# The state update of a head as one product over 128 rows: u and V share a tile, odd pairs put their outputs on the straight column half, and no state burst is cut in two

## The chip, the cores and the metric

The kernel runs on one core of a Trainium2 chip. The metric is the device time of one execution in microseconds. A core has a matrix engine (TensorE, "PE" in the profile, with its weight loads as "PEld"), a vector engine (VectorE, "DVE"), a scalar engine (ScalarE, "ACT"), a general one (GpSimd, "POOL"), and a sync engine (SyncE, "SP"), whose queue issues nearly all transfers of this kernel, in order. SBUF is the on-chip memory and PSUM the one that TensorE writes its sums to; both have 128 partitions.

## What is computed

One layer of a hybrid trunk for 512 tokens and 16 learned meta tokens ahead of them, width 2048. A normalised input goes through one projection whose columns feed two groups; group A has 16 heads of 64 with a recurrence over time, group B a gated convolution of width 3. Both are gated, go through one output projection, and the residual and a last norm follow. Cut to what matters here:

```python
Pr, Pc = (rmsnorm(h_res) @ w_in)[..., :RW_COLS], ...    # w_in: 2048 x 8320
# group A, for each head (N = 64), state S is N x N:
def step(S, inp):
    r_t, w_t, k_t, v_t, kk_t, b_t = inp
    sa = einsum('bhvk,bhk->bhv', S, kk_t)
    S = S * w_t[:, :, None, :] - sa[..., None] * b_t[:, :, None, :] + v_t[..., None] * k_t[:, :, None, :]
    y_t = einsum('bhvk,bhk->bhv', S, r_t)
    return S, y_t
y_a = (groupnorm(y) * lnx_g + lnx_b + bonus) * silu(g_r)
# group B
y_b = Bg * causal_conv_w3(Cg * hc) * silu(g_c)
out = rmsnorm(h_res + concat(y_a, y_b) @ w_out)
```

## The kernel before

**Tiles and stages.** The sequence is cut into 9 chunks of 64 (`NCH`): chunk 0 holds the meta tokens, 1 to 8 the real ones. The 16 heads are 8 pairs (`NPAIR`); a pair fills 128 partitions, head `h` the half `hs`, with `ho` for the other half. A pair i has the place `(i % 2) * 4 + i // 2`, so places 0 to 3 are the even pairs (e = 0) and 4 to 7 the odd ones (e = 1).

Instead of stepping through time, the kernel prepares each chunk of each head in closed form. `prepare` builds the operands of a pair, `invert` the inverse X of a triangular 64 x 64 matrix per chunk, and both write them to a tensor in device memory, `opd`, of one row per partition: 576 columns (`OPW`) hold AR, KK, BR, X, V and B' (offsets `O_AR` to `O_B`). V and B' come from transposes on VectorE (L922 and L824) whose 32 x 32 blocks are put in place by the transfers that `stash_later` issues (L902 to L908, L917 to L922, issued at L678). B' of a head has 128 rows, 64 that meet u and 64 that meet V, in two column pieces of 32 steps each, interleaved (`bb` in `recur`).

`recur` then runs the recurrence, chunk after chunk, all 16 heads at once. `load_chunk` (L1040) brings the operands of a chunk and a pair into the tile `ct`, 288 KB. For each chunk c:

- the products A·S and K·V into the PSUM tiles `z` (named rz; L1063), for even pairs in `z[0]` straight (rows and columns on the same half) and for odd pairs in `z[1]` crossed;
- ScalarE negates them into `pn` (L1071); filler for 2900 ns; the product with X (L1080) gives u in the other half of `z`; ScalarE and VectorE copy it to `u`, one each (L1083, L1084); filler for 2900 ns;
- the state burst. Its two lists are `here` and `there`. `here`: the state update into the PSUM tile `zs`, per head two products over 64 rows, B'·u and B'·V, straight (L1118); then, for the last odd pair, its three output products, into `z[0]`. `there`: the outputs `zy` of the other seven pairs, three products each (with the state, V and u), crossed (L1122). One step issues one entry of each list for both heads, so four products, one on each quadrant (a half of the rows with a half of the columns). In chunk 7 (`NCH - 2`) filler of 1000 ns is put in the middle of the burst. Chunk 0 has no outputs, chunk 8 no state update;
- the loads of chunk c+2 for the first four pairs (those of chunk c+1 for the other four stand behind `pn`); VectorE forms the new state (L1130, L1131); `norm` does the group norm of the outputs, seven heads of a column half from `zy` and one from `z[0]`, and writes them to `yd`; filler for 4200 + 1000 ns (4200 in chunk 7).

**What sets the order.** TensorE's order is the order of the code. `fill(ns)` takes as many matmuls of the input projection from the generator `mains` (tiles `ps_*`, L350 and L365) as last that many nanoseconds, and `until` takes them up to a certain result. So the projection's matmuls stand between all bursts of `prepare`, `invert` and `recur`. On the other engines a scheduler sorts by priority; `ahead()` lifts an instruction's priority. Weights of the projection come in halves of 512 KB into three buffers (`wr`, L157, on SP's queue); ScalarE casts each to a rounded high part (L149), VectorE subtracts to get the low part (L150), into six buffers (`w`), and TensorE takes them in turn. `later(ns, fn)` puts a transfer into the code once that much filler has been issued.

After the recurrence, `split_mix` reads `yd` back (the odd offset for the last place, L1207, is due to its straight outputs), and the output projection follows.

Of the kernel before, what the change touches and what calls it, by code (L numbers as in the profile page):

```python
# [89 lines left out]
def hymba_kernel(ctx: ExitStack, tc: tile.TileContext, xt, xtok, front, w_in, w_out, pv, lup, cst, msk, gf, out):  # L90
# [13 lines left out]
    opd = [dp.tile([NCH * P * OPW], F32, tag=f"opd{j}", name=f"opd{j}", bufs=1) for j in range(NPAIR)]  # L104
    rbd = [dp.tile([P, SEQ], F32, tag=f"rbd{j}", name=f"rbd{j}", bufs=1) for j in range(NPAIR)]
    gated = [dp.tile([P, SEQ], F32, tag=f"gated{j}", name=f"gated{j}", bufs=1) for j in range(NPAIR)]
    yd = dp.tile([2 * NPAIR * CH, SEQ], F32, tag="yd", name="yd", bufs=1)
    mixd = {j: dp.tile([P, SEQ], F32, tag=f"mixd{j}", name=f"mixd{j}", bufs=1) for j in range(NPAIR, KT)}

# [483 lines left out]
    def later(ns, fn):  # L593
        pending.append((clock[0] + ns, fn))
        pending.sort(key=lambda e: e[0])
# [89 lines left out]
    def stash_later(ns, *a):  # L685
        later(ns, lambda: stash(*a))
# [4 lines left out]
    def prepare(i):  # L691
# [209 lines left out]

        for h, hs, ho in heads:  # L902
            for b in range(2):
                for t in range(2):
                    stash_later(
                        9000 + 900 * (4 * h + 2 * b + t), i, bt[64 * h + 32 * b : 64 * h + 32 * b + 32, :, t].rearrange("p c s a -> p c (s a)"),
                        O_B + 64 * b, 64, 64 * h + 32 * t, 32, 0, NCH - 1,
                    )  # L908
# [7 lines left out]
        nc.vector.transpose(vs.rearrange("p c s -> p (c s)"), v)  # L916
        for b in range(4):  # L917
            for t in range(2):
                stash_later(
                    14000 + 1000 * (2 * b + t), i, vs[32 * b : 32 * b + 32, :, 32 * t : 32 * t + 32], O_V + 32 * (b % 2), 32,  # L920
                    64 * (1 - b // 2) + 32 * t, 32,
                )  # L922
        fill(FW["vt"])
        return dict(gt=gt, xT=xT, xo=xo, i=i)

# [112 lines left out]
            fill(FW["lev"] if level is level_a else FW["begin"])  # L1038

    def load_chunk(ch, c, pairs, ops):  # L1040
        n = OPW if c < NCH - 1 else O_B
        for i in pairs:
            t = ch.tile([P, OPW], F32, tag=f"ct{i}", name=f"ct{i}_{c}", bufs=2)
            nc.sync.dma_start(t[:, 0:n], spot(i, 0, P, c, 1, 1, 0, n))
            ops[c, i] = t

    def recur(ch):
        ops = {}  # L1050
        load_chunk(ch, 0, range(NPAIR), ops)
        load_chunk(ch, 1, range(NPAIR), ops)
        st = None
        for c in range(NCH):
            last = c == NCH - 1
            z = [pz.tile([P, 2, 4, CH], F32, tag="tz", name=f"rz{c}_{e}") for e in range(2)]
            for k in range(4):
                for part in range(0 if c else 1, 2):
                    for e in range(2):
                        t = ops[c, 2 * k + e]  # L1060
                        o = O_KK if part else O_AR
                        for h, hs, ho in heads:
                            nc.tensor.matmul(  # L1063
                                z[e][ho if e else hs, 0, k], t[hs, o : o + CH],
                                t[hs, O_V : O_V + CH] if part else st[hs, 4 * e + k],
                                start=(part == 0 or c == 0), stop=(part == 1),
                            )
            pn = ch.tile([P, 2, 4, CH], F32, tag="pn", name=f"pn{c}", bufs=2)
            with ahead():
                for e in range(2):  # L1070
                    nc.scalar.activation(pn[:, e], z[e][:, 0], AF.Copy, scale=-1.0)  # L1071
            if c and not last:
                load_chunk(ch, c + 1, range(4, NPAIR), ops)
            fill(FW["p"])
            for k in range(4):
                for e in range(2):
                    t = ops[c, 2 * k + e]
                    for h, hs, ho in heads:
                        m = ho if e else hs
                        nc.tensor.matmul(z[e][hs, 1, k], t[m, O_X : O_X + CH], pn[m, e, k], start=True, stop=True)  # L1080
            u = ch.tile([P, 2, 4, CH], F32, tag="u", name=f"u{c}", bufs=2)
            with ahead():
                nc.scalar.copy(u[:, 0], z[0][:, 1])  # L1083
                nc.vector.tensor_copy(u[:, 1], z[1][:, 1])  # L1084
# [6 lines left out]
            for k in range(4):  # L1091
                for e in range(2):
                    t, j = ops[c, 2 * k + e], 4 * e + k
                    if not last:
                        bb = t[:, O_B : O_B + 2 * CH].rearrange("p (s a) -> p a s", a=2)
                        here += [(zs, j, bb[:, 0], 0, u[:, e, k], 0, 2), (zs, j, bb[:, 1], 0, t[:, O_V : O_V + CH], 1, 2)]
                    if c and j < NPAIR - 1:
                        there += [
                            (zy, j, st[:, j], O_AR + CH, t, 0, 3),
                            (zy, j, t[:, O_V : O_V + CH], O_KK + CH, t, 1, 3),  # L1100
                            (zy, j, u[:, e, k], O_BR, t, 2, 3),
                        ]
                    elif c:

                        here += [
                            (z[0][:, 0], 0, t, O_AR + CH, st[:, j], 0, 3),
                            (z[0][:, 0], 0, t, O_KK + CH, t[:, O_V : O_V + CH], 1, 3),
                            (z[0][:, 0], 0, t, O_BR, u[:, e, k], 2, 3),
                        ]
            steps_ = max(len(here), len(there))  # L1110
            for n in range(steps_):
                if c == NCH - 2 and n == steps_ // 2:
                    fill(FW["mid"])
                if n < len(here):
                    d, j, t, o, x, a, b = here[n]
                    for h, hs, ho in heads:
                        w = t[hs, o : o + CH] if o else t[hs]
                        nc.tensor.matmul(d[hs, j], w, x[hs], start=(a == 0), stop=(a == b - 1))  # L1118
                if n < len(there):
                    d, j, x, o, t, a, b = there[n]  # L1120
                    for h, hs, ho in heads:
                        nc.tensor.matmul(d[ho, j], t[hs, o : o + CH], x[hs], start=(a == 0), stop=(a == b - 1))  # L1122
            if c + 2 < NCH:
                load_chunk(ch, c + 2, range(0, 4), ops)
            if not last:
                new = ch.tile([P, NPAIR, CH], F32, tag="st", name=f"st{c}", bufs=2)
                scale = dd[:, c].unsqueeze(2).to_broadcast([P, NPAIR, CH])
                with ahead():
                    if c:
                        nc.vector.tensor_tensor(out=new, in0=zs, in1=st, op=ALU.add)  # L1130
                    nc.vector.tensor_tensor(out=new, in0=new if c else zs, in1=scale, op=ALU.mult)  # L1131
                st = new
            if c:
                norm(ch, (zy, z[0][:, 0, 0:1]), c)
            fill(FW["s"] if c == NCH - 2 else FW["s"] + FW["mid"])


    def norm(ch, zs, c):
# [4 lines left out]
        def spread(j):  # L1143
            return nv[:, j].unsqueeze(2).to_broadcast([P, NPAIR, CH])

        for z, j in zip(zs, (slice(0, NPAIR - 1), slice(NPAIR - 1, NPAIR))):
# [49 lines left out]
    def split_mix(j):  # L1196
# [4 lines left out]
        if j < NPAIR:  # L1201
# [2 lines left out]
            nc.sync.dma_start(rb, rbd[j])  # L1204
            nc.sync.dma_start(gg, gated[j])
            for h, hs, ho in heads:
                o = ((1 - h if place[j] == NPAIR - 1 else h) * NPAIR + place[j]) * CH  # L1207
# [436 lines left out]
```

## Time and profile before

| what | value |
| --- | --- |
| runs | 997.5, 997.8, 995.52 us; median 997.5 |
| profiled execution | 996.79 us, of which the span of its instructions is 995.0 |
| granted TensorE clock, mean over the span | 0.997 |
| recurrence (630 to 770 us): TensorE busy | 138.31 of 140.00 us |
| same stretch: VectorE, ScalarE busy | 77.12 and 36.47 us |
| same stretch: DMA engines' share, rate | 0.69, 212 GB/s |
| from 836 us to the end (159.00 us): TensorE, VectorE busy | 150.80 and 140.85 us |

Lines of the profile name an engine, a line of the code and tiles as out<-in, with buffer numbers left out. Each float32 product of the program stands in the trace as two matmul records and two weight loads. "issue" as the thing waited for means that the engine waited for nothing that the profile shows. SPq and PEq are queues' own waits.

### The profile page before, as it was taken

The numbers are of one execution on the slowest core, as the hardware profiler recorded it, in microseconds if no ns is written. First come the engines' busy times: TensorE is split into PE (matmuls) and PEld (weight loads), VectorE is DVE, ScalarE is ACT, GpSimd is POOL, SyncE is SP. The second block draws the span as 40 slices with busy tenths as digits, with TensorE's granted clock in tenths as the row PEclk, the third lists the DMA queues.
The fourth block names the chain that finished last, engine by engine and source line by source line (L and its number), as shares of the span: only waits on it lengthen the run. The fifth ranks groups of instructions, "written<-read, shape, count | busy, mean of one in ns | idle before, by whom it ended". The sixth has DMA issues, their size and how long they took to land.

```text
span 995.0 us, 23811 instructions
## 1 busy us (share of the span) xinstructions
PE 984.1 (99%) x9767; PEld 911.1 (92%) x9767; DVE 706.1 (71%) x1404; ACT 389.8 (39%) x722; POOL 123.2 (12%) x234
## 2 busy tenths in 40 slices
PE   9999999999999999999999999999999999999996
PEld 9999999999998999999999989889789898788885
DVE  7777966578775778753778664455555697998896
ACT  7553432344313434322524322222222435546464
POOL 0110201112000111010111000011211102001001
PEclk9999999999999999999999999999999999999998
DMA  9436586245765375853365747987763698698654
GB/s 328 151 90 157 136 210 164 76 135 139 172 167 170 91 186 125 201 147 117 104 158 132 198 142 218 333 257 218 219 199 99 175 276 201 186 307 199 150 127 169
DMA packets 185148, 174.82 MB, mean 176 GB/s; under 512 B 121488, under 2 KB 142800, under 8 KB 184528
## 3 DMA queue, kind: packets, MB, share of 16 engines
q1 hardware_dynamic: 182448, 164.40, 57.6%
q0 software_dynamic: 2304, 8.39, 4.9%
q8 instruction: 76, 1.25, 0.5%
q10 hardware_dynamic: 288, 0.52, 0.1%
q14 instruction: 32, 0.26, 0.1%
HBM read 136.92 MB, written 36.35 MB: 174 GB/s over the span
## 4 chain that ended last, share of the span: by engine, by line
PE 95%; DVE 3%; issue 1%; ACT 0%; DMA 0%; DVEq 0%; POOL 0%; ACTq 0%
PE ps_v L350 9%; PE ps_h L350 9%; PE ps_C L350 9%; PE ps_g L350 9%; PE ps_B L365 9%; PE ps_gc L365 9%; PE ps_k L350 8%; PE ps_r L350 8%; PE M L1361 5%; PE P L1361 4%; PE Q L1361 2%; PE g L752 2%; PE ps_k L365 1%; DVE o L1330 1%; PE ps_r L365 1%; PE zs L1118 1%
## 5 line engine op out<-in xcount | busy, mean ns | idle before, releaser
L149 ACT CAST w<-wr 128x512 fp32r<-128x512 f32 x252 | 153.9, 619 | 283.1 <-PE ps_C L350 44.8
L150 DVE TENSOR_TENSOR w<-wr,w 128x512 fp32r<-128x512 f32 x252 | 176.8, 712 | 111.5 <-ACT w L149 106.3
L350 PE MATMUL ps_v<-xh,w 128*128 128x256 f32 (+2 forms) x512 | 84.0, 284 | 0.0
L365 PE MATMUL ps_B<-xh,w 128*128 128x512 f32 x256 | 83.4, 394 | 0.0
L350 PE MATMUL ps_h<-xh,w 128*128 128x256 f32 (+2 forms) x512 | 81.7, 281 | 0.0
L350 PE MATMUL ps_g<-xh,w 128*128 128x256 f32 (+2 forms) x512 | 81.5, 281 | 0.0
L365 PE MATMUL ps_gc<-xh,w 128*128 128x512 f32 x256 | 81.2, 392 | 0.0
L350 PE MATMUL ps_C<-xh,w 128*128 128x256 f32 (+2 forms) x512 | 80.8, 280 | 0.0
L350 PEld LDWEIGHTS ps_v<-xh,w 128*128 128x128 f32 x512 | 73.9, 188 | 0.3
L350 PE MATMUL ps_k<-xh,w 128*128 128x256 f32 (+1 forms) x448 | 73.4, 285 | 0.0
L350 PE MATMUL ps_r<-xh,w 128*128 128x256 f32 (+1 forms) x448 | 72.5, 280 | 0.0
L350 PEld LDWEIGHTS ps_h<-xh,w 128*128 128x128 f32 x512 | 72.1, 189 | 0.3
L350 PEld LDWEIGHTS ps_g<-xh,w 128*128 128x128 f32 x512 | 72.0, 189 | 0.4
L350 PEld LDWEIGHTS ps_C<-xh,w 128*128 128x128 f32 x512 | 71.7, 189 | 0.1
L350 PEld LDWEIGHTS ps_k<-xh,w 128*128 128x128 f32 x448 | 64.7, 188 | 0.4
L350 PEld LDWEIGHTS ps_r<-xh,w 128*128 128x128 f32 x448 | 63.5, 189 | 0.2
L350 PE MATMUL ps_h<-xl,w 128*128 128x256 f32 x256 | 57.4, 281 | 0.0
L365 PEld LDWEIGHTS ps_gc<-xh,w 128*128 128x128 f32 x256 | 47.8, 188 | 10.0
L365 PEld LDWEIGHTS ps_B<-xh,w 128*128 128x128 f32 x256 | 47.8, 188 | 9.7
L350 PE MATMUL ps_C<-xl,w 128*128 128x256 f32 x256 | 56.2, 280 | 0.0
L350 PE MATMUL ps_v<-xl,w 128*128 128x256 f32 x256 | 55.8, 278 | 0.0
L350 PE MATMUL ps_g<-xl,w 128*128 128x256 f32 x256 | 55.5, 278 | 0.0
(383 smaller groups left out, 2177.5 us busy)
## 6 DMA issues: line engine op xcount, KB each, us to landing
wr<-in_w_in_dram SPq DMA_DIRECT2D x126, 512.0 KB
ct<-opd SPq DMA_DIRECT2D x64, 288.0 KB
wo<-in_w_out_dram SPq DMA_DIRECT2D x24, 512.0 KB
x<-in_w_out_dram POOLq DMA_DIRECT2D x16, 512.0 KB, 5.9
opd<-ar SPq DMA_DIRECT2D x8, 576.0 KB
opd<-gt SPq DMA_DIRECT2D x16, 288.0 KB
opd<-bt SPq DMA_DIRECT2D x64, 64.0 KB
x<-in_w_out_dram SPq DMA_DIRECT2D x8, 512.0 KB
```

The costliest lines, as they stand in the source:

```text
L149: nc.scalar.copy(hi, rq)
L150: low[q] = eng.tensor_tensor(out=lo, in0=rq, in1=hi.bitcast(F32), op=ALU.subtract).ins
L350: nc.tensor.matmul(ps[r][:, 0 : b - a], ww[:, k * P : (k + 1) * P], xx[:, kt, a:b], start=(kt == 0 and n == 0), stop=(kt == KT - 1 and n = ...
L365: nc.tensor.matmul(ps[r], ww[:, w], xx[:, kt, a:b], start=(kt == 0 and n == 0), stop=(kt == KT - 1 and n == 2))
L752: nc.tensor.matmul(z[h][:, c - c0], bk[hs, c, h : h + 2, :].rearrange("p a s -> p (a s)"), ar[hs, c].rearrange("p a s -> p (a s)"), start= ...
L1118: nc.tensor.matmul(d[hs, j], w, x[hs], start=(a == 0), stop=(a == b - 1))
L1330: last = nc.vector.tensor_tensor(out=lo, in0=rq, in1=hi.bitcast(F32), op=ALU.subtract)
L1361: nc.tensor.matmul(bank[s], left(prod, jj, m, s), w, start=(jj == 0 and n == 0), stop=(jj == 7 and n == 2))
```

## The change

- V and B' leave the operand tile: `OPW` falls from 576 to 384 columns. They go to two tensors that all pairs share, `vd` and `bd`. The transfers that write them are as many as before (8 for each per pair); those of B' have runs of 32 elements now instead of 64, and the tile `bt` has whole rows of 64 instead of interleaved ones.
- `load_shared` loads, per chunk, V of all heads (`vn`, 256 KB), V once more as the second half of the rows of the tile `uv` (two transfers of 128 KB), and B' (`bw`, two of 256 KB). In chunk 8 only `vn` is loaded. It stands where `load_chunk` stands at the end of a chunk.
- u is copied into `uv` beside V: two copies of 64 partitions each on ScalarE and on VectorE.
- The state update is one product per head over 128 rows, `bw` with `uv`, onto one half of the columns, 16 in all, and they stand ahead of the outputs.
- Outputs: even pairs crossed into `zy`, odd pairs straight into `z[0]`, one product of each of the four quadrants after another.
- Chunk 7's burst isn't cut. `norm` reads four heads from `zy` and four from `z[0]`, and the offset into `yd` follows the place.

```diff
-OPW = 9 * CH
-O_AR, O_KK, O_BR, O_X, O_V, O_B, O_K = 0, 128, 256, 320, 384, 448, 512
+OPW = 6 * CH
+O_AR, O_KK, O_BR, O_X = 0, 128, 256, 320
...
-        bt = cq.tile([P, NCH - 1, 2, CH // 2, 2], F32, tag="bt", name=f"bt{i}")
+        bt = cq.tile([P, 2, NCH - 1, CH], F32, tag="bt", name=f"bt{i}")
         for a in range(2):
-            nc.vector.transpose(bt[:, :, :, :, a], bk[:, 0 : NCH - 1, a].rearrange("p c (t s) -> p c t s", t=2))
+            nc.vector.transpose(bt[:, a], bk[:, 0 : NCH - 1, a])
...
+    def load_shared(ch, c, ops):
+        n = CH * NPAIR * CH
+        vn = ch.tile([P, NPAIR, CH], F32, tag="vn", name=f"vn{c}", bufs=2)
+        uv = ch.tile([P, 2, NPAIR, CH], F32, tag="uv", name=f"uv{c}", bufs=2)
+        bw = ch.tile([P, NPAIR, 2, CH], F32, tag="bw", name=f"bw{c}", bufs=2)
+        nc.sync.dma_start(vn, vd[2 * c * n : (2 * c + 2) * n].rearrange("(s j d) -> s j d", j=NPAIR, d=CH))
+        for h, hs, ho in heads:
+            if c < NCH - 1:
+                nc.sync.dma_start(
+                    uv[ho, h], vd[(2 * c + h) * n : (2 * c + h + 1) * n].rearrange("(s j d) -> s j d", j=NPAIR, d=CH)
+                )
+                nc.sync.dma_start(
+                    bw[hs].rearrange("p j h d -> p (j h d)"),
+                    bass.AP(
+                        tensor=bd.tensor, offset=bd.offset + (4 * c + h) * 32 * NPAIR * P,
+                        ap=[[64 * NPAIR * P, 2], [NPAIR * P, 32], [1, NPAIR * P]],
+                    ),
+                )
+        ops[c] = vn, uv, bw
...
-            u = ch.tile([P, 2, 4, CH], F32, tag="u", name=f"u{c}", bufs=2)
             with ahead():
-                nc.scalar.copy(u[:, 0], z[0][:, 1])
-                nc.vector.tensor_copy(u[:, 1], z[1][:, 1])
+                for h, hs, ho in heads:
+                    nc.scalar.copy(uv[hs, h, 0:4], z[0][hs, 1])
+                    nc.vector.tensor_copy(uv[hs, h, 4:8], z[1][hs, 1])
             fill(FW["u"])
-            here, there = [], []
             if not last:
                 zs = pi.tile([P, NPAIR, CH], F32, tag="misc", name=f"zs{c}")
+                for k in range(4):
+                    for e in range(2):
+                        j = 4 * e + k
+                        for h, hs, ho in heads:
+                            nc.tensor.matmul(zs[hs, j], bw[:, j, h], uv[:, h, j], start=True, stop=True)
             if c:
-                zy = pi.tile([P, NPAIR - 1, CH], F32, tag="ser", name=f"zy{c}")
...
-            steps_ = max(len(here), len(there))
-            for n in range(steps_):
-                if c == NCH - 2 and n == steps_ // 2:
-                    fill(FW["mid"])
...
+                zy = (pi.tile([P, 4, CH], F32, tag="ser", name=f"zy{c}"), z[0][:, 0])
+                for k in range(4):
+                    for n in range(3):
+                        for e in range(2):
+                            t, j = ops[c, 2 * k + e], 4 * e + k
+                            for h, hs, ho in heads:
+                                o = (O_AR + CH, O_KK + CH, O_BR)[n]
+                                x = (st[hs, j], vn[hs, j], uv[hs, h, j])[n]
+                                nc.tensor.matmul(
+                                    zy[e][hs if e else ho, k], t[hs, o : o + CH], x, start=(n == 0), stop=(n == 2)
+                                )
             if c + 2 < NCH:
                 load_chunk(ch, c + 2, range(0, 4), ops)
+                load_shared(ch, c + 2, ops)
...
-            fill(FW["s"] if c == NCH - 2 else FW["s"] + FW["mid"])
+            fill(FW["s"] + FW["mid"])
```

TensorE's queue where the state burst of chunk 1 begins, behind the last filler product (ps_B). The shape is the output's; x2 stands for the two heads. Before:

```order
L365 MATMUL ps_B_0_8550<-xl,w_8300 128x512
L1118 MATMUL zs_8658<-u_8641,ct_1_8336 64x64 x2
L1122 MATMUL zy_8659<-st_8495,ct_1_8336 64x64 x2
L1118 MATMUL zs_8658<-ct_1_8336 64x64 x2
L1122 MATMUL zy_8659<-ct_1_8336 64x64 x2
L1118 MATMUL zs_8658<-u_8641,ct_1_8338 64x64 x2
L1122 MATMUL zy_8659<-u_8641,ct_1_8336 64x64 x2
```

And the same place of the changed kernel:

```order
L367 MATMUL ps_B_0_8561<-xl,w_8302 128x512
L1122 MATMUL zs_8670<-uv_8363,bw_8364 64x64 x16
L1132 MATMUL zy_8687<-st_8506,ct_1_8346 64x64 x2
L1132 MATMUL rz_0_8569<-st_8506,ct_1_8348 64x64 x2
L1132 MATMUL zy_8687<-vn_8362,ct_1_8346 64x64 x2
L1132 MATMUL rz_0_8569<-vn_8362,ct_1_8348 64x64 x2
L1132 MATMUL zy_8687<-uv_8363,ct_1_8346 64x64 x2
```

The state update stood in every second row and now stands in one block of 16 products ahead; the outputs of even (zy) and odd pairs (rz_0) alternate behind it.

SP's queue at the end of chunk 0, where the operands of chunk 2 are loaded (wr is a half tile of weights, rb and gg belong to the stage behind the recurrence). Before:

```order
L157 DMA wr_8389<-in_w_in_dram 128x1024
L157 DMA wr_8542<-in_w_in_dram 128x1024
L1204 DMA rb_10840<-rbd_78 128x512
L1205 DMA gg_10841<-gated_86 128x512
L157 DMA wr_8608<-in_w_in_dram 128x1024
L1044 DMA ct_2_8487<-opd_70 128x576
L1044 DMA ct_2_8489<-opd_71 128x576
L1044 DMA ct_2_8491<-opd_72 128x576
L1044 DMA ct_2_8493<-opd_73 128x576
L1044 DMA ct_2_8595<-opd_74 128x576
```

And now:

```order
L159 DMA wr_8407<-in_w_in_dram 128x1024
L1053 DMA ct_2_8490<-opd_70 128x384
L1053 DMA ct_2_8492<-opd_71 128x384
L1053 DMA ct_2_8494<-opd_72 128x384
L1053 DMA ct_2_8496<-opd_73 128x384
L1061 DMA vn_8498<-vd 128x512
L1064 DMA uv_8499<-vd 64x512
L1067 DMA bw_8500<-bd 64x1x1024
L1064 DMA uv_8499<-vd 64x512
L1067 DMA bw_8500<-bd 64x1x1024
L159 DMA wr_8553<-in_w_in_dram 128x1024
L1053 DMA ct_2_8606<-opd_74 128x384
```

Five transfers of the shared tiles stand behind the first four loads of ct, and the next weight load, which stood ahead of all of them, stands behind.

More of the change, by code (lines that the diff above doesn't have):

```diff
@@ L903, in prepare @@
             for b in range(2):
[L904 to L908, printed above, removed]
+                for a in range(2):
+                    later(9000 + 900 * (4 * h + 2 * b + a), lambda h=h, b=b, a=a: nc.sync.dma_start(
+                        bass.AP(
+                            tensor=bd.tensor,
+                            offset=bd.offset + (h ^ a) * 32 * NPAIR * P + place[i] * P + 64 * h + 32 * b,
+                            ap=[[NPAIR * P, 32], [64 * NPAIR * P, 2 * NCH - 2], [1, 32]],
+                        ),
+                        bt[64 * h + 32 * b : 64 * h + 32 * b + 32, a].rearrange("p c (t s) -> p (c t) s", s=32),
+                    ))
         until("v", i)
@@ L918, in prepare @@
             for t in range(2):
[L919 to L922, printed above, removed]
+                later(14000 + 1000 * (2 * b + t), lambda b=b, t=t: nc.sync.dma_start(
+                    bass.AP(
+                        tensor=vd.tensor,
+                        offset=vd.offset + (64 * (1 - b // 2) + 32 * t) * NPAIR * CH + place[i] * CH + 32 * (b % 2),
+                        ap=[[NPAIR * CH, 32], [P * NPAIR * CH, NCH], [1, 32]],
+                    ),
+                    vs[32 * b : 32 * b + 32, :, 32 * t : 32 * t + 32],
+                ))
         fill(FW["vt"])
@@ L1064, in recur @@
                                 z[e][ho if e else hs, 0, k], t[hs, o : o + CH],
-                                t[hs, O_V : O_V + CH] if part else st[hs, 4 * e + k],
+                                vn[hs, 4 * e + k] if part else st[hs, 4 * e + k],
                                 start=(part == 0 or c == 0), stop=(part == 1),
@@ L1085, in recur @@
             fill(FW["u"])
-            here, there = [], []
             if not last:
                 zs = pi.tile([P, NPAIR, CH], F32, tag="misc", name=f"zs{c}")
-            if c:
-                zy = pi.tile([P, NPAIR - 1, CH], F32, tag="ser", name=f"zy{c}")
[L1091 to L1109, printed above, removed]
@@ L1110, in recur @@
-            steps_ = max(len(here), len(there))
-            for n in range(steps_):
-                if c == NCH - 2 and n == steps_ // 2:
-                    fill(FW["mid"])
[L1114 to L1122, printed above, removed]
+                for k in range(4):
[3 more added lines that the diff above has]
+                            nc.tensor.matmul(zs[hs, j], bw[:, j, h], uv[:, h, j], start=True, stop=True)
@@ L1133, in recur @@
             if c:
-                norm(ch, (zy, z[0][:, 0, 0:1]), c)
-            fill(FW["s"] if c == NCH - 2 else FW["s"] + FW["mid"])
+                norm(ch, zy, c)
+            fill(FW["s"] + FW["mid"])
     def norm(ch, zs, c):
@@ L1144, in spread @@
             return nv[:, j].unsqueeze(2).to_broadcast([P, NPAIR, CH])
-        for z, j in zip(zs, (slice(0, NPAIR - 1), slice(NPAIR - 1, NPAIR))):
+        for z, j in zip(zs, (slice(0, 4), slice(4, NPAIR))):
             nc.vector.tensor_reduce(out=nv[:, 0, j], in_=z, op=ALU.add, axis=AX.X)
@@ L1206, in split_mix @@
             for h, hs, ho in heads:
-                o = ((1 - h if place[j] == NPAIR - 1 else h) * NPAIR + place[j]) * CH
+                o = ((1 - h if place[j] >= 4 else h) * NPAIR + place[j]) * CH
                 nc.sync.dma_start(raw[hs], yd[o : o + CH])
```

13 lines of the change are left out of this document (9 added, 4 removed).

## The prediction

> **What bounds the kernel now.** First the page: who is busy, when, at what clock, and which chain ended last.
>
> ```profile
> span 995.0 us, 23811 instructions
> PE 984.1 (99%) x9767; PEld 911.1 (92%) x9767; DVE 706.1 (71%) x1404; ACT 389.8 (39%) x722; POOL 123.2 (12%) x234
> PE   9999999999999999999999999999999999999996
> PEclk9999999999999999999999999999999999999998
> PE 95%; DVE 3%; issue 1%; ACT 0%; DMA 0%; DVEq 0%; POOL 0%; ACTq 0%
> ```
>
> TensorE is busy in every slice but the last, at full clock, and 95% of the chain that ended last is its work: what changes is the time of its queue. Then the view of its waits, which is all of three rows:
>
> ```profile
> PE zy L1122 <- issue: 1.7, 1, 1.7
> PE pwarm L200 <- DVE cold L197: 1.0, 1, 1.0
> PE M L1361 <- DVE o L1330: 0.3, 1, 0.3
> ```
>
> No transfer and no evacuation holds TensorE up anywhere. So an edit counts by the time that it takes or gives on TensorE, unless it makes a new wait. The first row, 1.7 us in which the queue waited for nothing that is recorded, lies inside a burst that the change rewrites.
>
> **The bursts as they stand.** I read the edited bursts from TensorE's timeline (start, duration, engine, line, tile, shape, count), from the first product of a burst to the first filler product behind it. Chunk 0, where the outputs aren't wanted:
>
> ```profile
> 630.33 0.34 PE L1118 MATMUL zs<-u,ct 64*64 64x64 f32 x4
> 632.18 0.29 PE L1118 MATMUL zs<-ct 64*64 64x64 f32 x4
> 632.40 0.50 PE L350 MATMUL ps_h<-xl,w 128*128 128x256 f32 x2
> ```
>
> 2.07 us for 16 steps of two products (each has two records, its two passes); the first row to the second is 15 steps and a bit, 0.12 us each, so about 0.15 us is entry and exit. Chunk 1, which chunks 2 to 4 and 6 repeat within 0.01 us:
>
> ```profile
> 646.71 0.28 PE L1118 MATMUL zs<-u,ct 64*64 64x64 f32 x2
> 649.32 0.50 PE L365 MATMUL ps_B<-xh,w 128*128 128x512 f32 x1
> ```
>
> 2.61 us for 21 steps. What a step on all four quadrants takes is shown by the products of L1063:
>
> ```profile
> 638.35 0.30 PE L1063 MATMUL rz<-ct 64*64 64x64 f32 x8
> 639.05 0.30 PE L1063 MATMUL rz<-ct 64*64 64x64 f32 x8
> ```
>
> Six steps of four products in 0.70 us: 0.117 us. 21 x 0.117 + 0.15 = 2.61, so the burst of now is 21 such steps and nothing else. Chunk 5 has the stall, chunk 7 is cut in two, chunk 8 has outputs alone:
>
> ```profile
> 714.14 0.28 PE L1118 MATMUL zs<-u,ct 64*64 64x64 f32 x2
> 718.33 0.27 PE L1122 MATMUL zy<-st,ct 64*64 64x64 f32 x3 [1.69 <-issue]
> 718.83 0.50 PE L365 MATMUL ps_gc<-xl,w 128*128 128x512 f32 x1
> 749.80 0.28 PE L1118 MATMUL zs<-u,ct 64*64 64x64 f32 x2
> 751.16 0.39 PE L350 MATMUL ps_h<-xl,w 128*128 128x256 f32 x1
> 752.44 0.28 PE L1118 MATMUL zs<-u,ct 64*64 64x64 f32 x2
> 753.88 0.39 PE L350 MATMUL ps_h<-xl,w 128*128 128x256 f32 x1
> 767.13 0.27 PE L1118 MATMUL rz<-st,ct 64*64 64x64 f32 x2
> 769.74 0.50 PE L365 MATMUL ps_B<-xh,w 128*128 128x512 f32 x1
> ```
>
> Chunk 5: 4.69 us, 2.08 over the regular burst. Chunk 7: 1.36 + 1.44 = 2.80. Chunk 8: 2.61, though half its products are gone: the three products of an odd pair stand on the same two quadrants as the rest for most of it.
>
> **The new bursts, priced.** Outputs: 48 products in order of the four quadrants, 12 steps x 0.117 = 1.40 us; the step is measured, only the place is new. State update: 16 products over 128 rows, each on half of the columns. No row of this kernel has that shape. Nearest is the block of the key norm, 128 rows on a quarter of the columns:
>
> ```profile
> 83.90 0.16 PEld L784 LDWEIGHTS ps_v<-sq,cs 128*32 128x32 f32 x8
> 83.91 0.45 PE L784 MATMUL ps_v<-sq,cs 128*32 128x144 f32 x8
> 84.29 0.40 PE L763 MATMUL ps_v<-ar,bk 64*128 64x16 f32 x4
> ```
>
> Its eight weight loads start and end within 0.16 us, while its products run, and the whole block with its change of form at the end takes 0.38 us. So column tiles of full height don't stand in line for one another. Per pair of heads I take the two-quadrant step, 0.12 us (two products, one behind each other's load, as in chunk 0). Bounds: below, 0.107, a tenth under it, as half the instructions carry the same work; above, twice, 0.24, the case where the two halves of the columns go one after the other. I take 0.12, because the key-norm row is nearest in form. Two forms in a burst need a change between them: the 0.38 us of the key-norm block hold two rounds of products (eight on four quarters), 0.24 at 0.12 each, which leaves 0.14.
>
> - Chunk 0: 8 x 0.12 + 0.15 = 1.11, from 2.07: -0.96.
> - Chunks 1 to 6: 8 x 0.12 + 1.40 + 0.15 + 0.14 = 2.65, from 2.61: +0.04 each, +0.26 in all.
> - Chunk 7, whole again: 2.65 from 2.80: -0.15.
> - Chunk 8: 1.40 + 0.15 = 1.55, from 2.61: -1.06.
>
> Sum: -1.9 us. A third fewer products of the state burst give little in six of nine chunks, since before two quadrants worked on the state while the other two worked on outputs.
>
> **The stall.** Its chunk has the same instructions as its neighbours; during it the DMA view of that microsecond shows a fetch of instructions:
>
> ```profile
> q8 instruction: 1, 0.02, 5.9%
> ```
>
> The old burst asks for 80 products and their loads, in two passes 320 instructions, within 2.61 us; the new one 64 products, 256 instructions, and the first 64 of these take 0.96 us. A thinner stretch at the front gives a fetch more time, and one burst in eight met it before. I take the 2.08 us as gone; the ends are 0 (it stays or falls on another burst) and -2.1.
>
> **What is hidden, and by what.** u leaves PSUM in four copies of 64 partitions instead of two of 128. TensorE has filler from 660.10 to 663.50:
>
> ```profile
> 660.10 0.50 PE L365 MATMUL ps_gc<-xl,w 128*128 128x512 f32 x1
> 660.20 0.37 ACT L1083 COPY u<-rz 128x256 f32<-128x256 f32 x1 [0.17 <-PE rz L1080]
> 660.67 0.42 DVE L1084 COPY u<-rz 128x256 f32<-128x256 f32 x1
> 663.50 0.28 PE L1118 MATMUL zs<-u,ct 64*64 64x64 f32 x2
> ```
>
> The last copy ends at 661.09; another of at most 0.42 ends at 661.5, 2 us before it is wanted. Without the filler it would cost 0.42 x 9 = 3.8. The norm reads 4 + 4 heads instead of 7 + 1, and the transposes into bt write whole rows where they wrote every second element: as many instructions and elements as before on an engine that is idle for 29% of the span, so nothing.
>
> DMAs: B' is written in 64 transfers as before, with runs of 128 B in place of 256 B. The same queue writes V in runs of 128 B already:
>
> ```profile
> L678 SPq DMA_DIRECT2D opd<-bt x64: 303/466/1369, 95.2 to 564.8; - x64
> L678 SPq DMA_DIRECT2D opd<-vs x64: 303/453/1415, 101.6 to 575.2; - x64
> SPq L157 <- DVE w L150: 302.9, 76, 11.3
> ```
>
> The issue takes the same half microsecond for both; doubled for B' it would be 0.47 x 64 = 30 us on a queue that stands still for 302.9 us behind weights that nobody needs yet. In the recurrence each chunk loads 8 x 192 KB + 1 MB instead of 8 x 288 KB, 0.26 MB more, in five issues more:
>
> ```profile
> 623.53 1.08 SPq L157 DMA_DIRECT2D wr<-in_w_in_dram  x2
> 630.21 0.33 SPq L157 DMA_DIRECT2D wr<-in_w_in_dram  x1
> 630.83 5.21 SPq L1044 DMA_DIRECT2D ct<-opd  x8
> 640.00:680.00 40.00, 40.00 (x714) 34.35 (x713) 21.75 (x38) 10.88 (x22) 5.37 (x5) 1.00 0.79 244
> ```
>
> In the last row, of the windows (the DMA engines' share is 0.79, at 244 GB/s), 0.26 MB is 1.1 us of a chunk of 16.4 (630.33 to 646.71). The shared loads of chunk c+2 wait for the burst of chunk c, as four of the eight ct loads do now, and behind them stands a weight load that stood ahead. The second load of 623.53 is the one that slips, to 636 at the latest; TensorE first reads what comes of it in the filler that begins at 660.10, so over 20 us cover it. The loads themselves are wanted one and a half chunks on: the products of L1063 begin over 8 us ahead of a state burst (638.35, 646.71), in chunk 2 at about 655, 23 us behind 632.40. If that cover were gone, a chunk would wait up to the 5.2 us that eight loads take to issue.
>
> **Sum.** 995.0 of span and 1.8 around it are the 996.79 of the profiled execution. -1.9 - 2.1 = -4.0: 992.8; the median of the runs shown is 0.7 higher, so 993.5. TensorE has no wait behind the recurrence either, up to the one of 0.3 us, so the gain should reach the end.
>
> **Rivals.**
>
> *The stall stays, moves, or the gain is lost later.* Then -1.9 alone: 995.6. For it: one fetch more or less is luck of position. And here the engines run level:
>
> ```profile
> 840.00:880.00 40.00, 39.73 (x174) 32.13 (x173) 39.24 (x51) 23.01 (x39) 3.46 (x4) 1.00 0.72 192
> ```
>
> VectorE is busy for 39.24 of 40 us; if it, not TensorE, sets the pace there, up to all of the gain stays in that stretch (997.5). Against it: TensorE is 39.73 busy, with the 0.3 us wait alone.
>
> *Column tiles one after the other (slower).* At 0.24 a pair of heads the state update is 1.92 us. Chunks 1 to 6: 0.24 x 8 + 1.40 + 0.29 = 3.62, +1.01 each, +6.05; chunk 7 +0.82; chunk 0 at 2.07, 0; chunk 8 -1.06: +5.8. With the stall as before or gone, 1003.3 or 1001.2. It decides from 0.15 a pair on if the stall stays (64 pairs x 0.03 = 1.9), from 0.18 if it goes. Against it are the eight loads of the key norm within 0.16 us.
> The Trainium skill, "TensorE: Matmul & The Clock Gate", in its part on packing small matmuls (what overlaps and what doesn't), has the rule for this: a weight load runs beside a matmul in flight only if the two differ in their row group, which two column tiles of full height never do. By that rule the sum would be the 1003.3; the key-norm rows here speak against it.
>
> *A hidden wait on the loads (slower).* The bursts of chunks 2 to 7 find vn, uv or bw not landed, or the weights queued behind them come late. It decides once a transfer lands over 20 us behind the burst that releases it; from there each chunk loses what five more issues add, 5 x 0.33 = 1.7 us. Three to six such chunks: 993.5 + 5 to 10 = 998.6 to 1003.7. For it: one queue in order, with five more transfers behind one burst. Against it: the cover of 20 and 23 us, and that no wait for a transfer is in TensorE's list now.
>
> *It doesn't do what it says.* The products fall from 8010 to 7882 in the order, 128 as meant; I give this nothing.
>
> **Chances.** Forecast, 993.5 with its own range 992 to 994.8: 0.47. Saving alone or lost later, 995.6, to 998: 0.30. Column tiles slow, 1001 to 1004, or part of the way: 0.10. Hidden wait: 0.10. The rest, a second stall removed or added: 0.03. The range holds the first two and the lower half of the next: 991 to 1001. A measurement of this kernel tells 0.3%, 3 us, from no change: faster under 994.5, slower over 1000.5. Faster is the forecast without its upper edge and a little of the second case, 0.48; slower is the two slow rivals without their low ends, 0.15; the same, 0.37.
>
> **What would show it.** Right: bursts of 1.1 us (chunk 0), 2.6 to 2.7 (1 to 7) and 1.55 (8), and a row of waits of TensorE without "issue" between 630 and 770. Bursts of 3.6 us with zs taking 1.9 show the column tiles serial; a wait of TensorE on a DMA of vn, uv, bw or on a cast shows the hidden wait; bursts as priced with TensorE's waits on VectorE past 836 show the gain lost later. It is wrong if the bursts agree and the span doesn't.

## The result

The changed kernel takes 1061.86 us (median of 4 runs, 1060.28 to 1063.01) against 997.65 us (median of 4): the ratio is 1.0646, with a 95% interval of 1.0624 to 1.0668. It is slower by 64 us where 993.5 was forecast, far outside 991 to 1001. With only the form of one kind of load changed, it takes 992.64 us, and then every burst is within 0.03 us of what the sum said (experiment 1).

The page of the changed kernel, in the lines that were shown of before:

```profile
span 1060.2 us, 23372 instructions
PE 999.8 (94%) x9511; PEld 923.1 (87%) x9511; DVE 708.6 (67%) x1413; ACT 392.0 (37%) x731; POOL 123.9 (12%) x234
PE   9999999999999999999999986785959999999997
PEclk9999999999999999999999997888888999999999
DMA  9427484375852758533778455556567488688654
```

The first 23 slices of TensorE's row are as before, and so are the last ones. Between them lie slices with holes, and about there the granted clock is lower. DMA has 4 to 7 tenths there, so the transfer engines as a whole aren't full. The windows by stage (us; busy time of PE, PEld, DVE, ACT, POOL; clock; DMA share; GB/s) fence it in:

```profile
80.00:580.00 500.00, 500.00 (x4833) 483.87 (x4832) 353.87 (x807) 177.37 (x322) 60.83 (x141) 1.00 0.60 151
630.00:770.00 140.00, 102.92 (x1540) 89.28 (x1541) 45.02 (x84) 23.02 (x48) 13.07 (x14) 0.84 0.56 158
```

Up to 580 us TensorE has no gap: the new stores of V and B' are hidden. In the recurrence it is idle for 37 of 140 us. What it waits for:

```profile
PE zs L1122 <- ACT uv L1113: 23.8, 2, 13.3
PE rz L1093 <- issue: 13.7, 8, 3.8
PE rz L1110 <- ACT pn L1101: 8.6, 1, 8.6
PE zs L1122 <- DMA bw<-bd: 5.1, 1, 5.1
```

For the second row, 13.7 us at the products with the state, the trace names no cause, and it stays open. Two of the rows name ScalarE, an engine that is busy for 37% of the span. Its own wait (7.0 us in the kernel of experiment 1), and the chain of waits for one of these holes (start, duration, what), say why it was late:

```profile
ACT w L151 <- DMA wr<-in_w_in_dram: 111.5, 11, 25.8
```

```profile
616.61 11.93 DMA bw<-bd
628.56 9.10 DMA ct<-opd
637.75 16.58 DMA wr<-in_w_in_dram
654.46 0.48 issue
654.95 0.61 ACT w L151
655.56 0.62 ACT cv L486
656.21 0.39 ACT pn L1101
656.64 1.40 PE rz L1110 x32
```

A load of bw takes 11.93 us to land, the ct loads and a load of weights queue up behind it, the weights 16.58 us. ScalarE's next instruction is the cast of those weights; pn, which TensorE needs, stands behind the cast on ScalarE's queue. SyncE's queue, which issues these loads, stands still for them too, at the group norm's stores (L1176) and at bw's own loads (L1067):

```profile
SPq L1176 <- DMA bw<-bd: 25.5, 7, 6.8
SPq L1067 <- DMA bw<-bd: 22.5, 4, 6.2
```

In the kernel of experiment 1, waits of this queue for bw come to 1.2 us. How much of the loss these waits make beyond the late landings themselves wasn't separated. Now the view of the transfers in 648 to 655 us, cut into 40 slices:

```profile
DMA  7489995574111200111111111111101111111111
GB/s 176 176 328 363 316 269 94 70 105 70 35 23 23 47 23 23 47 47 70 70 47 47 47 47 47 47 47 70 70 32 50 50 41 44 53 53 44 44 53 53
bw<-bd SPq DMA_DIRECT2D x2, 256.0 KB
```

In the last 5 us of it all 16 engines together are about one tenth busy. As a window (the last two numbers are share and GB/s):

```profile
650.00:655.00 5.00, 0.00 (x0) 0.00 (x0) 0.00 (x0) 0.58 (x2) 0.00 (x0) 0.76 0.13 48
```

A share of 0.13 is two engines of 16 (0.125), at some 24 GB/s each. Two loads of bw had been issued at 636.04 and 637.13 and the weights behind them at 637.75, and the weights land in this stretch; the x2 in the view are the next two loads of bw, issued at 653.08 and 654.87. Each bw load is written as [2, 32, 1024], two blocks of 32 rows; the other loads of the recurrence have 64 or 128 rows as their outermost dimension.

Of the 69.3 us between this execution (1060.2) and that of experiment 1 (990.9), 18.3 are longer busy time of TensorE (999.8 against 981.5) and 51 are idle. The longer busy time is the clock: it is 0.50 in seven stretches that begin in or right behind a wait, and TensorE is busy for 35.9 us in them, half of which is 18.0. Two of the seven, and the state update in three bursts:

```profile
632.14:638.97 6.83, 4.34 (x43) 4.25 (x44) 0.69 (x1) 0.00 (x0) 0.00 (x0) 0.50 0.45 141
734.54:748.20 13.66, 3.75 (x60) 3.18 (x64) 3.80 (x7) 2.39 (x5) 0.00 (x0) 0.50 0.65 152
```

```profile
634.63 2.06 PE L1122 MATMUL zs<-uv,bw 128*64 128x64 f32 x32 [5.08 <-DMA bw<-bd]
...
663.65 1.15 PE L1122 MATMUL zs<-uv,bw 128*64 128x64 f32 x32
...
744.45 3.08 PE L1122 MATMUL zs<-uv,bw 128*64 128x64 f32 x32 [13.30 <-ACT uv L1113]
744.85 0.87 DVE L1114 COPY uv<-rz 64x256 f32<-64x256 f32 x2
```

The same 32 records take 1.15 us in a full stream and 2.06 behind a wait of 5 us, at the clock of 0.50. The 3.08 behind the wait of 13 us aren't the clock alone: VectorE's copies of u, which the odd pairs need, end at 745.72, in the middle of the row.

### The profile page after: what moved, and what is told of

Read it like the earlier page. It is cut to its first block, busy times and chain, and to the rows that moved or that the text cites. A ratio compares the mean times of both kernels' runs of the same rounds, so it can differ in the third digit from the quotient of the medians.

```text
span 1060.2 us, 23372 instructions
## 1 busy us (share of the span) xinstructions
PE 999.8 (94%) x9511; PEld 923.1 (87%) x9511; DVE 708.6 (67%) x1413; ACT 392.0 (37%) x731; POOL 123.9 (12%) x234
## 4 chain that ended last, share of the span: by engine, by line
PE 83%; DMA 11%; DVE 3%; issue 1%; ACT 1%; SPq 1%; DVEq 0%; POOL 0%; ACTq 0%
PE ps_v L352 9%; PE ps_g L352 9%; PE ps_B L367 8%; PE ps_k L352 8%; PE ps_r L352 7%; PE ps_gc L367 7%; PE ps_h L352 7%; PE ps_C L352 6%; DMA wr<-in_w_in_dram 5%; PE M L1374 5%; PE P L1374 3%; DMA ct<-opd 3%; DMA bw<-bd 2%; PE Q L1374 2%; PE g L754 1%
## 5 line engine op out<-in xcount | busy, mean ns | idle before, releaser
L152 DVE TENSOR_TENSOR w<-wr,w 128x512 fp32r<-128x512 f32 x252 | 174.6, 704 | 185.6 <-ACT w L151 184.4
```

What stands on the lines that cost most here:

```text
L152: low[q] = eng.tensor_tensor(out=lo, in0=rq, in1=hi.bitcast(F32), op=ALU.subtract).ins
```

## The experiments

Theories. *Form*: a load whose outermost dimension counts 2 is carried by two of the 16 engines, and what else these two must carry comes late. *Volume*: 0.26 MB and five transfers more per chunk are too much. *Order*: the weights stand behind loads that wait for the burst.

**1. bw in four loads of [32, 1024] (992.64 us), and in two of [64, 1024] (993.54).** The first keeps bytes, addresses and order and adds two transfers per chunk:

```diff
-                nc.sync.dma_start(
-                    bw[hs].rearrange("p j h d -> p (j h d)"),
-                    bass.AP(
-                        tensor=bd.tensor, offset=bd.offset + (4 * c + h) * 32 * NPAIR * P,
-                        ap=[[64 * NPAIR * P, 2], [NPAIR * P, 32], [1, NPAIR * P]],
-                    ),
-                )
+                for t in range(2):
+                    nc.sync.dma_start(
+                        bw[64 * h + 32 * t : 64 * h + 32 * t + 32].rearrange("p j h d -> p (j h d)"),
+                        bass.AP(
+                            tensor=bd.tensor, offset=bd.offset + (4 * c + h + 2 * t) * 32 * NPAIR * P,
+                            ap=[[NPAIR * P, 32], [1, NPAIR * P]],
+                        ),
+                    )
```

> Each load of bw (two per chunk, of [2, 32, 1024] elements) is made as two of [32, 1024]: same bytes, same addresses, two transfers more per chunk. Theory 'form': in the changed kernel the DMA engines' share falls to one tenth at 49 to 50 GB/s for 5 to 10 us behind each pair of bw loads, as if two of the 16 engines carried all of it; with an outermost dimension of 32 the bw loads land in 2 to 3 us, TensorE has no wait but 'issue', and the time is the 993.5 of the sum, 992 to 996. Theory 'volume' (0.26 MB and five transfers more per chunk are what the queue can't take): seven transfers more, so 1062 or worse. Theory 'order' (the weight load stands behind the loads that wait for the burst): nothing changes, 1055 to 1065.

The second reads 64 rows in one block:

```diff
-                        tensor=bd.tensor, offset=bd.offset + (4 * c + h) * 32 * NPAIR * P,
-                        ap=[[64 * NPAIR * P, 2], [NPAIR * P, 32], [1, NPAIR * P]],
+                        tensor=bd.tensor, offset=bd.offset + (2 * c + h) * 64 * NPAIR * P,
+                        ap=[[NPAIR * P, 64], [1, NPAIR * P]],
```

> The bw loads read 64 rows that follow one another, [64, 1024], instead of two blocks of 32: as many transfers and bytes as in the changed kernel, in another form (the rows of B' are then not those that belong to u and V, so the state update is another sum; no time hangs on the values). 'Form': 992 to 996, shares of DMA of 0.6 or more behind the burst. 'Volume' and 'order': 1055 to 1065.

With [32, 1024], in 5 runs, the ratio to the kernel before is 0.9955 (0.9941 to 0.9968): 4.8 us or half a per cent faster, small but outside the interval. This is its whole list of TensorE's waits, and its window:

```profile
PE pwarm L202 <- DVE cold L199: 1.0, 1, 1.0
PE M L1375 <- DVE o L1344: 0.3, 1, 0.3
```

```profile
630.00:770.00 140.00, 140.00 (x2437) 123.56 (x2436) 80.82 (x151) 38.93 (x81) 21.18 (x25) 1.00 0.81 228
```

No hole in the recurrence, at a DMA share of 0.81 and 228 GB/s. More transfers, as many bytes and the same order are harmless, so volume and order alone fall. [64, 1024] reads rows that don't belong to u and V, so its results aren't the layer's; as many transfers as in the changed kernel took 993.54 us with it. In the kernel with [32, 1024] the rest of the change can be read undisturbed, below.

**2. The same load in the kernel before, read by nobody.** Two loads of 256 KB per chunk into a spare tile, in two forms:

```diff
+                dm = ch.tile([P, 1024], F32, tag="dm", name=f"dm{c}", bufs=2)
+                for h, hs, ho in heads:
+                    nc.sync.dma_start(
+                        dm[hs],
+                        bass.AP(
+                            tensor=opd[0].tensor, offset=opd[0].offset + 32768 * h,
+                            ap=[[64 * 1024, 2], [1024, 32], [1, 1024]],
+                        ),
+                    )
```

> The kernel before, and at the end of chunks 0 to 6 two loads of [2, 32, 1024] (256 KB each) into a tile that nobody reads. If what costs is that these hold up the transfers queued behind them: 20 to 60 us slower, 1017 to 1060, with TensorE waiting on u or pn behind a cast. If it is that the state burst itself waits for bw: no more than 'volume' gives, 3.5 MB at 200 GB/s beside other work, 997 to 1003.

and with `ap=[[1024, 64], [1, 1024]]`:

> As the run before, with the two loads in the form [64, 1024]: same bytes, number and place. 'Form': 997 to 1000. 'Volume': as slow as the run before.

[2, 32, 1024] took 1041.99 us, [64, 1024] 995.81. Since nobody reads the tile, 44.6 us (over 997.41) are what these loads do to others. Apart from [32, 1024], each kernel of these experiments was run once, and the kernel before took 997.41 us beside experiments 1 and 2, 999.77 beside 3 and 4 and 996.24 beside 5 to 7, so a difference of 3 us tells nothing. In the longest rows of its list TensorE waits for ct and for ScalarE:

```profile
PE rz L1063 <- DMA ct<-opd: 9.9, 20, 2.4
PE rz L1080 <- ACT pn L1071: 6.0, 3, 3.5
PE zs L1118 <- ACT u L1083: 5.5, 2, 3.1
```

**3. How many engines: [4, 16, 1024] (1011.13 us) and [8, 8, 1024] (997.59) in place of [2, 32, 1024], the rest as in experiment 2.**

```diff
-                            ap=[[64 * 1024, 2], [1024, 32], [1, 1024]],
+                            ap=[[32 * 1024, 4], [1024, 16], [1, 1024]],
```

> The kernel before with the two idle loads per chunk, now as [4, 16, 1024]. In the changed kernel two engines moved 49 to 50 GB/s together, so 24.6 each. If as many engines carry a load as its outermost dimension counts: four, 512 KB in 5.3 us, about 98 GB/s in the stretches where nothing else moves; of the 16.4 us of a chunk the busiest engines then need 5.3 for these loads and some 8.6 for their 16th of the other transfers (3.4 MB per chunk, 0.21 MB at 24.6 GB/s), which fits, so 996 to 1004. If any load of three dimensions is slow: 1035 to 1045 as with [2, 32, 1024]. The Trainium skill, 'DMA: Bandwidth & Descriptors', in the section on why a DMA increments its semaphore by 16, has the first of these as its rule (the largest count up to 16 that divides the slowest dimension of both sides).

> As [8, 8, 1024]. Engines as the outermost dimension: eight, 512 KB in 2.7 us, so 995 to 998, as with [64, 1024]. Any three dimensions slow: 1035 to 1045.

Three dimensions as such aren't slow; 2, 4, 8 and 64 as the outermost count give 44.6, 13.7, 0.2 and -1.6 us over 997.41. Stretches in which little but the idle loads moves count the engines, here with [4, 16, 1024] and with [8, 8, 1024]:

```profile
658.00:660.50 2.50, 2.50 (x41) 1.88 (x40) 2.21 (x4) 0.71 (x2) 0.12 (x1) 1.00 0.25 96
644.50:647.00 2.50, 2.50 (x12) 1.79 (x10) 0.69 (x1) 0.62 (x1) 0.00 (x0) 1.00 0.49 182
```

A share of 0.25 is four engines and 0.49 eight, where it was 0.13 with [2, 32, 1024]: in these three as many engines as the outermost count.

[4, 16, 1024] fell between the two ranges that were expected. The expectation took the other work of an engine from bytes, 8.6 us of a chunk; the share of the windows, 0.66 of 17.2, makes it 11.4. A busy engine moved less there than the 24.6 GB/s of the expectation (198 GB/s at a share of 0.66 are 19 each); why wasn't tried.

**4. Only one head's bw in the bad form (1023.45 us); bw from ScalarE's queue (1056.42).** The first keeps the load of [2, 32, 1024] for h = 1 and takes experiment 1's for h = 0, the second replaces `nc.sync.dma_start` by `nc.scalar.dma_start` for bw.

> The changed kernel with the bw load of the second head as it is, [2, 32, 1024], and that of the first as two of [32, 1024]. Two engines then have about 5.2 + 7.8 + 0.6 = 13.6 us of work per chunk of 16.4. If more work than time on two engines is the cause, nearly all of the loss goes: 992 to 1000. If each such load costs what stands behind it: half of the 69 us stays, 1020 to 1035.

> The changed kernel with the bw loads as they are, but issued from ScalarE's queue. If the cost is that what SP's queue issues behind them stands in line: most of it goes, 993 to 1005. If it is that two engines have more work than time (10.5 us for bw and some 7.8 us for their 16th of the rest, 18.3 in a chunk of 16.4), whatever queue it comes from: at least 8 x 1.9 = 15 us slower than the 993 that it would be, 1008 to 1062.

SP's order of issue is not the cause, since another queue brings back only 5 us; SyncE's queue goes on waiting for bw's landings there, 23.7 us at L1053 alone. The half cost half, which was put down as the other theory's number; but that rested on the low figure for the other work as well. With it mended, the account of the busiest engine got one more test.

**5. One idle load of [2, 32, 1024] per chunk in the kernel before (1009.12 us).** `for h, hs, ho in heads[:1]:` in experiment 2.

> The kernel before with one idle load of [2, 32, 1024] per chunk instead of two. Account of the busiest engine: the windows show all engines 0.66 to 0.69 busy in the kernel before, 11.3 us of a chunk of 16.4 to 17; one such load adds 5.3 us on two engines, 16.6, as two loads of [4, 16, 1024] did on four (1011.13). Two of [2, 32, 1024] made it 21.8 and the chunk took 23.7. So 1005 to 1016. If each such load costs the same whatever else is there: half of the 44.6 of two, 1017 to 1022.

It fell in the range of the account, with [4, 16, 1024] x 2, which gives the busiest engine as much. All runs together: work per chunk of the busiest engine (512 KB take two engines 10.7 us at 49 GB/s, or 5.3 for half; the others' from the DMA share times the chunk, 11.4 before, 12.2 with the changed loads, as if spread evenly over the 16), against the mean chunk in the trace, from chunk 1's state burst to chunk 8's:

| run | slow loads | others | sum, us | chunk, us |
| --- | --- | --- | --- | --- |
| before | 0 | 11.4 | 11.4 | 17.2 |
| [8, 8, 1024] x 2 | 2.7 | 11.4 | 14.1 | 17.2 |
| [4, 16, 1024] x 2 | 5.3 | 11.4 | 16.7 | 19.2 |
| [2, 32, 1024] x 1 | 5.3 | 11.4 | 16.7 | 19.0 |
| changed, one head mended | 6.0 | 12.2 | 18.2 | 19.9 |
| [2, 32, 1024] x 2 | 10.7 | 11.4 | 22.1 | 23.7 |
| changed | 10.7 | 12.2 | 22.9 | 24.3 |

TensorE needs 16.9 us for a chunk. At 14.1 nothing is lost, and from 18.2 on the chunk follows the busiest engine, 1.4 to 1.7 us longer. The two rows at 16.7 don't fit, since they lose 2 us where the account has room, and their agreement is no proof of it. The idle loads aren't issued once a chunk, since nothing waits for them; with one per chunk all seven are issued between 623.37 and 672.83 us, these among them:

```profile
638.50 0.54 SPq L1127 DMA_DIRECT2D dm<-opd  x1
639.96 10.39 SPq L1127 DMA_DIRECT2D dm<-opd  x2
656.43 0.50 SPq L1127 DMA_DIRECT2D dm<-opd  x1
```

And 9.0 of the 13.7 us of [4, 16, 1024] are three stalls of TensorE with no recorded cause (more below). So the account holds where the two engines have clearly more work than time; where it starts was not shown.

**6. bw from GpSimd's queue (1065.46 us): inconclusive.** As in 4, with `nc.gpsimd.dma_start`.

> The changed kernel, its bw loads in the form [2, 32, 1024] as they are, but issued from GpSimd's queue. From ScalarE's queue the same loads gave 1056.42, so SP's order isn't it. If the form as such is slow, or the two engines are the same whatever queue issues: 1045 to 1065. If the cost is that always the same two engines carry them, and this queue takes others in turn: 992 to 1000, since a bw load has 20 us and more. The Trainium skill, 'DMA: Bandwidth & Descriptors', in the section on why a DMA increments its semaphore by 16, says that the sync engine's queue takes the lowest-numbered engines and GpSimd's takes consecutive ones from a cursor that goes round.

It can't tell whether that queue takes other engines in turn, because GpSimd itself is held up. It stands idle for 13 us on average ahead of ten of the sixteen loads, and the norm waits for it (13.8 us in all in the changed kernel). Its timeline (start, duration, idle before), and VectorE's wait in the norm:

```profile
638.50 0.65 POOL L1067 DMA_DIRECT2D bw<-bd  x1 [12.19 <-issue]
639.16 0.21 POOL L406 TENSOR_TENSOR u<-ex 128x2 f32<-128x2 f32 x1
653.67 0.69 POOL L1067 DMA_DIRECT2D bw<-bd  x1 [14.30 <-issue]
668.38 0.65 POOL L1067 DMA_DIRECT2D bw<-bd  x1 [14.02 <-issue]
```

```profile
DVE yc L1171 <- POOL nv L116: 52.9, 8, 14.0
```

What stands behind a load starts at once (639.16); the idle time lies ahead of the next load.

**7. The state update among the outputs instead of ahead of them (1011.69 us).** In the kernel of experiment 1, the two products of one head pair's update stand behind each of the first two groups of four output products:

```diff
+                        if n < 2 and not last:
+                            update(n, k)
```

> The changed kernel with its bw loads as [32, 1024] (992.64), and the 16 products of the state update put between the output products instead of ahead of them: two behind each four of the first two terms of a pair of pairs. If each change between products of 128 and of 64 rows costs the 0.14 us that the sum has for one: 16 changes instead of one, bursts of 2.64 + 15 x 0.14 = 4.7 us in chunks 1 to 7, so 992.6 + 14.7 = 1007. If a product of 128 rows only takes its place in the row: bursts of 2.5 to 2.7, 992 to 993.

```profile
645.67 0.27 PE L1138 MATMUL zy<-st,ct 64*64 64x64 f32 x2
...
645.95 0.34 PE L1123 MATMUL zs<-uv,bw 128*64 128x64 f32 x4
646.21 0.27 PE L1138 MATMUL zy<-vn,ct 64*64 64x64 f32 x2
...
650.62 0.73 PE L367 MATMUL ps_B<-xh,w 128*128 128x512 f32 x2
```

The burst of chunk 1 takes 4.95 us (645.67 to 650.62) instead of 2.64. It has 16 changes of form instead of one: (4.95 - 2.64) / 15 = 0.154 us for each, as a mean of both ways, 0.14 in the sum; with 15 changes in each of 7 chunks it is 16.2 of the 19.0 us. TensorE waits on weights for another 2.7.

## Why the prediction was wrong, and where it was right

**The step that failed** is the one on the shared loads under "what is hidden, and by what": "0.26 MB is 1.1 us of a chunk". It priced the loads by bytes at the mean rate of all 16 engines (244 GB/s) and by what SP takes to issue them. Two of the five, 512 KB of the 1 MB, go over two engines at 49 GB/s: 10.7 us of a 16.9 us chunk, on engines that have about 12.2 us of other work in it. The covers of 20 and 23 us were real but are for a single late load; they don't help where two engines fall behind by 6 us in every chunk. The weights then land late, the cast holds ScalarE's queue, and pn and u stand behind it. The rival "a hidden wait on the loads" named the place and the way, weights behind the loads, but its price, 1.7 us a chunk from five issues, was four times too small (24.3 - 16.9 = 7.4), and with it its chance. The Trainium skill, "DMA: Bandwidth & Descriptors", in the section on why a DMA increments its semaphore by 16 (how many engines), has the rule that was missed: a transfer runs on the largest number up to 16 that divides the count of the slowest dimension on both sides. The runs with 2, 4, 8 and 64 agree with it.

The rest is read from experiment 1, where nothing is late. Its bursts (first product, first row of outputs, next filler):

```profile
630.39 1.15 PE L1123 MATMUL zs<-uv,bw 128*64 128x64 f32 x32
631.47 0.50 PE L352 MATMUL ps_h<-xl,w 128*128 128x256 f32 x2
```

```profile
645.85 1.15 PE L1123 MATMUL zs<-uv,bw 128*64 128x64 f32 x32
646.93 0.27 PE L1133 MATMUL zy<-st,ct 64*64 64x64 f32 x2
...
648.49 0.73 PE L367 MATMUL ps_B<-xh,w 128*128 128x512 f32 x2
```

```profile
764.09 0.27 PE L1133 MATMUL zy<-st,ct 64*64 64x64 f32 x2
...
765.65 0.73 PE L367 MATMUL ps_B<-xh,w 128*128 128x512 f32 x2
```

| burst | before | sum | measured |
| --- | --- | --- | --- |
| chunk 0 | 2.07 | 1.11 | 1.08 |
| chunks 1 to 6 | 2.61 | 2.65 | 2.64 |
| chunk 7 | 2.80 | 2.65 | 2.64 |
| chunk 8 | 2.61 | 1.55 | 1.56 |
| chunk 5's stall | 2.08 | 0 | 0 |
| end of chunk 8's burst | 769.74 | -4.0 | 765.65, so -4.09 |

- **Column tiles.** 16 products with their 32 weight loads take 1.08 us with the change of form behind, so under 0.12 us a pair where the rival had 0.24. The rival of 1003 and the rule named beside it don't hold for products of this form here.
- **The stall.** It is gone in experiment 1, but the reason given isn't shown. In the kernel before with two [64, 1024] loads the burst has its old density, and chunk 5 takes 2.88 us, 0.27 over; with [8, 8, 1024] a stall of 1.7 is back, in chunk 4. With the new burst and [64, 1024] some bursts still take 2.83 and 3.16. So it moves with the transfers' timing, and that the 2.1 us forecast for it came out is luck as far as the runs show. The fetch of instructions, which the prediction named, does stand by it. Before, one ends at 716.90 us and TensorE goes on at 718.33, 1.43 us later; in the kernel before with idle loads, eleven of the thirteen stalls of TensorE without a recorded cause end 1.2 to 1.6 us behind the end of a fetch. That speaks for a wait on the fetch, but no experiment was made on it.
- **Two readings.** "A third fewer products of the state burst" is a fifth, 64 instead of 80; the sum didn't use it. The chunk of 16.4 us is chunk 0's; from there on a chunk is 17.2 us before and 16.9 in experiment 1.
- **Gain lost later.** None: -4.09 at the end of the recurrence and -4.1 in the span (995.0 to 990.9). VectorE, at 39 of 40 us there, didn't hold it.
- **Copies, norm, stores.** Four copies of 64 partitions take 0.37 and 0.42 us each, as those of 128 did, beside filler; no TensorE wait names them once the loads are mended. B' stores issue in 0.51 us (median; 0.55 in the changed kernel) instead of 0.47 and cost nothing.

## What to carry to other kernels

Price a transfer by how many engines carry it: read the outermost count of both access patterns before the bytes (the runs here vary the source's alone), and add up the work of the busiest engine per period, not the mean of 16. A mean DMA share of 0.56 hid two engines here with 22.9 us of work in a chunk of 24.3. A load that nobody waits for can stop TensorE by way of a queue in order: follow what stands behind the wait on each engine. And where two tile forms share a burst, sort them: a change cost 0.15 us here.

## What the runs showed of the hardware

- Where little else moves, loads of [2, 32, 1024] go at 47 to 53 GB/s and a share of 0.13 to 0.16, whether SP or ScalarE issues them (1061.86 and 1056.42 us). With several on their way the share stays there (0.13 and 52 GB/s at 651 to 655 us in experiment 2), so they use the same two engines. From GpSimd's queue it is 0.14 and 44 GB/s (670.0 to 676.5 us in experiment 6).
- On GpSimd's queue the engine stood idle for 13 us on average ahead of ten of sixteen such loads (129.9 us in all); an instruction behind a load started at once.
- Around a wait of 5 or 13 us TensorE's granted clock was 0.50, for 4 us or so beyond the end of the wait (to 638.97 and 748.20 us); here this was 18 us of 69.
